# Two modulation chunks moved to the end of the experts, modulation started during the last merges, output weights loaded later

## The chip, the cores and the metric

The kernel runs on one core of a Trainium2 chip. The core has a matrix engine (TensorE, PE in the profile), a vector engine (VectorE, DVE), a scalar engine (ScalarE, ACT), GpSimd (POOL) and SyncE (SP). Each has its own queue of instructions, taken in order, and they meet through semaphores; 16 DMA engines move data between the core's memory and DRAM. SP issues most of the loads here, POOL the modulation's. The metric is device microseconds for one execution, as the median of several.

## The reference, cut to what matters

Two layers work on 512 latent and 256 context tokens of width 1024. All is float32; the kernel splits the operands of its large products into a high and a low part and adds three products.

```python
m_lat = jnp.split((sc @ ada_w[i] + ada_b[i])[:, None, :], 6, axis=-1)   # sc = silu(c)
m_ctx = jnp.split(scc @ ada_w[i] + ada_b[i], 6, axis=-1)                 # scc = silu(c_ctx)
h = modulate(rms_norm(x, norm_mix_w[i]), m[0], m[1])
y = hybrid_mixer(h)           # attention heads | gated delta rule, both ways; then @ w_out
x = x + m[2] * y
h = modulate(rms_norm(x, norm_ffn_w[i]), m[3], m[4])
x = x + m[5] * hier_moe(h)    # 32 experts, each token in two of them
```

`ada_w[i]` is 1024 x 6144 floats, 24 MB for a layer. The six chunks of 1024 columns are the m[0] to m[5] above. They depend on `c` and `c_ctx` alone, so they can be computed at any time before they are used: chunks 0 and 1 at the start of their layer, chunk 2 behind the mixer, 3 and 4 behind it, 5 behind the experts.

## The kernel before, in words

A layer runs in these stages, which the times of the first execution place as follows.

1. **Norm and input projection.** `norm_mix` modulates the tokens, transposes them and splits them into `hh` and `hl`. Products with the streamed `w_in` give `pn` (gates `gev`, queries, keys) and `pt` (delta rule's inputs). In layer 1 this begins at about 1112 us.
2. **Chunks and merges.** Each chunk of the delta rule needs the inverse of a small triangular matrix. It is built from 32x32 blocks; `merge_batch` joins them: 16 products of 32x32 into `mg` (L847), a ScalarE copy (L848), 16 products of the other kind (L851), a ScalarE copy into `xm` (L852), twice over, and a store of `xad`. The last merges stand directly ahead of the loop.
3. **The loop of 12 steps** (about 393 to 606 us in layer 0, 1461 to 1628 in layer 1). `delta_step` carries the state of the recurrence; `pz` (L917) is a step's first product. Each step's data (`lk`, `lx`, `lq`) are loaded one step ahead by SP; `lx` is multiplied with `lq` on POOL. Strings of letters (`PAT`) say in which order a step (d), slots of attention (f: scores `sc`, softmax `pp`, transposes `ptr`, product `pv`) and parts of the modulation (a) are written down. From that order and from its own model a scheduler sets each engine's order, which is then fixed.
4. **The tail**: output projection with `w_out` (raw loads `wr`, high parts `woh`), residual, norm, router.
5. **The experts**: 32 of them, weights streamed by SP three ahead through four buffers `w13` and two for the second matrix. Each result `ey` is added to `yd` in DRAM by an indirect DMA of POOL. Behind the last one the kernel branches over code for full experts, and the next layer loads `x` from `yd`.

**Modulation.** `ada_steps` does a chunk in four parts. A part (`ada_part`) loads 1 MB of `ada_w` into one of two buffers `araw` on POOL's queue, multiplies it on TensorE (8 products that the trace shows as 16, into `aps`), and copies the first part's sum on ScalarE or adds the others on VectorE (`ac`). After the fourth part the bias `ab` is added and the chunk stored to DRAM (`md`, L283), from where later stages load it. Layer 0's loop does chunks 2 to 5 of layer 0 and chunks 0 and 1 of layer 1, 24 parts; layer 1's loop does chunks 2 to 5 of layer 1, 16 parts, of which the scheduler puts one in front of the loop.

`WS` is the step from which on the raw output weights are loaded, one after each step, three in the loop; in the built order all three stand together behind the second steps' loads.

## Time and profile before

| | us |
|---|---|
| runs of the kernel before | 2085.26, 2092.97, 2104.73; median 2092.97 |
| profiled execution, its own time | 2092.51 |
| span of the profile | 2090.7 |
| TensorE busy | 1763.9 (84%) |
| VectorE busy | 1460.2 (70%) |
| ScalarE busy | 1016.6 (49%) |
| POOL busy | 868.6 (42%) |
| DMA | 427.81 MB, mean 205 GB/s |

The rows are read thus. A row of a timeline gives start, duration, engine, line, operation, what it writes <- what it reads, and how many instructions stand together; in brackets follow the idle time of that engine just before and what ended it. A row of waits adds such idle times by what ended them. A table of stretches gives each engine's busy time, the number of instructions and the granted clock of TensorE as a share of full speed. Idle time of one engine matters only where others wait for that engine.

### The profile page before, as it was taken

To read this page: it belongs to the slowest core of one execution; us is meant where nothing else is said; L and a number is where in the kernel's file an instruction comes from. 1 tells how busy PE (TensorE), PEld (TensorE's weight loads), DVE (VectorE), ACT (ScalarE), POOL (GpSimd) and SP (SyncE) were. 2 spreads that over 40 slices of the span, in tenths; PEclk is the share of its full clock that TensorE was granted. 3 is DMA by queue.
4 is the path that set the end of the run, shared out by engine and by line. 5 is a ranking of instruction groups with operands and counts; after the bars stand their busy time and mean duration, and the time that the engine had idled before them with its cause. 6 is when DMAs were issued, how large, how long until landed. Compare 5 with 4: busy or idle time off the path is not lost. (4 is left out here: it accounts for less than half of the span.)

```text
span 2090.7 us, 35600 instructions
## 1 busy us (share of the span) xinstructions
PE 1763.9 (84%) x13835; PEld 1382.1 (66%) x13835; DVE 1460.2 (70%) x2472; ACT 1016.6 (49%) x1595; POOL 868.6 (42%) x915
## 2 busy tenths in 40 slices
PE   6998798978877879999996987776898577999994
PEld 4887687766656746666665866675676465777773
DVE  4469996567673668887874579992678465787774
ACT  3444344665541246565554543343566225666663
POOL 4456653234354423343226466650234443334321
PEclk9999897799998979999997998875899788999997
DMA  9222445798645389998853323445983558988872
GB/s 283 74 71 82 129 119 166 218 259 246 205 125 144 147 327 336 332 322 301 324 161 119 97 73 97 131 130 158 282 233 83 148 214 315 346 334 330 328 295 102
DMA packets 227687, 427.81 MB, mean 205 GB/s; under 512 B 83720, under 2 KB 157180, under 8 KB 202939
## 3 DMA queue, kind: packets, MB, share of 16 engines
q1 hardware_dynamic: 171547, 329.09, 47.1%
q0 software_dynamic: 33536, 72.59, 12.2%
q10 hardware_dynamic: 22432, 23.81, 3.3%
q8 instruction: 111, 1.82, 0.4%
q14 instruction: 61, 0.50, 0.1%
HBM read 386.82 MB, written 84.67 MB: 226 GB/s over the span
## 5 line engine op out<-in xcount | busy, mean ns | idle before, releaser
L1418 POOL DMA_INDIRECT yd<-ey,idx x64 | 114.2, 1784 | 425.3 <-DMA yd<-ey,idx 151.8
L1364 PE MATMUL pab<-w,xt 128*128 128x512 f32 x512 | 230.3, 592 | 0.0
L1332 ACT ACTIVATE w2h<-w 128x2048 fp32r<-128x2048 f32 x64 | 122.7, 1917 | 134.5 <-PE py L1406 83.3
L1333 DVE TENSOR_TENSOR w2l<-w,w2h 128x2048 fp32r<-128x2048 f32 x64 | 146.8, 2294 | 53.5 <-ACT w2h L1332 52.9
L1333 DVE TENSOR_TENSOR w13l<-w,w13h 128x2048 fp32r<-128x2048 f32 x64 | 146.5, 2288 | 28.9 <-ACT w13h L1332 28.9
L1364 PEld LDWEIGHTS pab<-w,xt 128*128 128x128 f32 x512 | 93.0, 191 | 92.0 <-issue 91.8
L489 POOL TENSOR_TENSOR wlo<-wraw,whi 128x1024 fp32r<-128x1024 f32 (+1 forms) x44 | 111.1, 2529 | 93.1 <-ACT whi L488 93.1
L239 PE MATMUL pn<-whi,hh 128*128 128x256 f32 (+1 forms) x432 | 134.6, 314 | 16.3 <-ACT gev L1562 12.5
L239 PE MATMUL po<-woh,m 128*128 128x512 f32 x320 | 114.1, 434 | 30.7 <-ACT woh L1069 14.5
L239 PE MATMUL pn<-whi,hl 128*128 128x256 f32 (+1 forms) x432 | 135.3, 316 | 2.0 <-DVE hl L350 1.7
L239 PE MATMUL pn<-wlo,hh 128*128 128x256 f32 (+1 forms) x432 | 132.4, 308 | 1.2 <-POOL wlo L489 1.2
L1332 ACT ACTIVATE w13h<-w 128x2048 fp32r<-128x2048 f32 x64 | 121.8, 1902 | 6.4 <-DMA w<-w 4.1
L239 PE MATMUL pt<-hh,wlo 128*128 128x512 f32 (+1 forms) x352 | 124.2, 353 | 0.0
L239 PE MATMUL pt<-hh,whi 128*128 128x512 f32 (+1 forms) x352 | 122.9, 349 | 0.0
L239 PE MATMUL pt<-hl,whi 128*128 128x512 f32 (+1 forms) x352 | 122.2, 347 | 0.0
L1406 PE MATMUL py<-w2h,gh 128*128 128x512 f32 x256 | 109.1, 426 | 4.6 <-DVE ey L1413 4.4
L1337 POOL DMA_INDIRECT xe<-h2d,idx x64 | 85.9, 1343 | 61.2 <-issue 22.9
L518 DVE SCALAR_TENSOR_TENSOR dT<-xin,cw,dT 128x772 f32<-128x772 f32 x64 | 80.1, 1252 | 43.3 <-ACT dT L516 41.5
L1406 PE MATMUL py<-w2h,gl 128*128 128x512 f32 x256 | 103.1, 403 | 7.8 <-DVE gl L1385 7.8
L1413 DVE TENSOR_TENSOR ey<-py,eg 128x1024 f32<-128x1024 f32 x64 | 78.2, 1222 | 44.1 <-PE py L1406 37.8
L239 PEld LDWEIGHTS pn<-whi,hh 128*128 128x128 f32 x432 | 90.6, 211 | 23.2 <-ACT gev L1562 13.5
L1348 PEld LDWEIGHTS xt<-cst,xe 128*128 128x128 f32 x512 | 68.3, 192 | 55.1 <-issue 29.8
(401 smaller groups left out, 5124.4 us busy)
## 6 DMA issues: line engine op xcount, KB each, us to landing
w<-w SPq DMA_DIRECT2D x192, 1024.0 KB, 9.8
araw<-ada_w POOLq DMA_DIRECT2D x40, 1024.0 KB, 6.8
wraw<-w_in SPq DMA_DIRECT2D x40, 512.0 KB, 4.1
lk<-vk SPq DMA_DIRECT2D x48, 256.0 KB, 7.2
lx<-xad SPq DMA_DIRECT2D x40, 256.0 KB, 10.0
araw<-ada_w SPq DMA_DIRECT2D x8, 1024.0 KB, 10.9
wr<-w_out SPq DMA_DIRECT2D x8, 1024.0 KB, 13.4
vk<-vr ACTq DMA_DIRECT2D x16, 384.0 KB, 3.7
```

The costliest lines, as they stand in the source:

```text
L239: self.nc.tensor.matmul(ps, a(k), b(k), start=(first and n == 0), stop=(last and n == 3 * nk - 1))
L489: getattr(nc, eng).tensor_tensor(lo, raw, hi, op=OP.subtract)
L518: nc.vector.scalar_tensor_tensor(dst, xin[:, tap:tap + 772], cw[:, tap, f:f + 1], dst, op0=OP.mult, op1=OP.add)
L1332: self.pin(nc.scalar.activation(hi, src, AF.Copy))
L1333: self.pin(nc.vector.tensor_tensor(lo, src, hi, op=OP.subtract))
L1337: self.pin(self.nc.gpsimd.indirect_dma_start(out=xe, out_offset=None, in_=h2d, in_offset=bass.IndirectOffsetOnAxis(ap=idx, axis=0), bounds ...
L1348: pin(nc.tensor.transpose(ps[:, k * P:(k + 1) * P], xe.rearrange("p (q k) -> p k q", k=8)[:, 4 * q + k, :], self.ident))
L1364: self.pin(self.nc.tensor.matmul(out, xt[:, k, :], w13[:, :, KS + k, :], start=False, stop=(k == 3)))
L1406: pin(self.nc.tensor.matmul(py[:, n * 512:(n + 1) * 512], a[:, j, :], b[:, c], start=(j + m == 0), stop=(j == 1 and m == 2)))
L1413: pin(nc.vector.tensor_tensor(y, py, gates, op=OP.mult))
L1418: self.pin(self.nc.gpsimd.indirect_dma_start(out=yd, out_offset=bass.IndirectOffsetOnAxis(ap=idx, axis=0), in_=y, in_offset=None, bounds_c ...
```

## The change

It has three parts.

**`LATE = (2, 3)`.** Chunks 2 and 3 of layer 1 are no longer done in layer 1's loop. `ada_late` does them at the end of layer 0's experts: four loads of 2 MB each, as two of 1 MB, into the experts' `w13` buffers on SP's queue, issued as experts 28 to 31 release theirs; 64 products (eight parts' worth) into one tile, chunk 3 two rows below chunk 2 through a shifted copy of the small operand (`scs`); one ScalarE copy `la`. Two of the eight parts stand ahead of the last expert's second product, six behind it and ahead of the branch. `ada_close` then adds the biases in layer 1, behind `norm_mix`: for each chunk a small load `lb` (SP), a VectorE sum, a store to `md` (POOL). `md_row` finds chunk 3 two rows lower.

**`PRE = (6, 8)`.** Before the loop, six of layer 0's parts and all eight that are left in layer 1's are written down, so that the scheduler can place them beside the last merges. The strings `PAT` are the same; an "a" of an exhausted sequence does nothing.

**`WS = 7`.** The raw output weights are loaded from step 7 on, and each behind that step's `lx` load.

```diff
-WS = 4
+WS = 7
+PRE = (6, 8)
+LATE = (2, 3)
...
+    def ada_late(self, i, chs, pool, load):
...
+        acc = self.late_sum = pool.tile([P, UNIT], F32, tag="la", name="la")
...
+        for ch in chs:
+            for n in range(2):
+                raws.append(load(src[:, 4 * n:4 * n + 4, ch * D:(ch + 1) * D]))
+                yield
+        ps = self.psC("aps")
+        for j in range(2):
+            for k in range(8):
+                if k % 2 == 0:
+                    yield
+                for g in range(4):
+                    w = raws[2 * j + k // 4][:, k % 4, g * UNIT:(g + 1) * UNIT]
+                    self.pin(self.nc.tensor.matmul(ps[32 * g:32 * g + 32, :UNIT], self.scs[j][:, k, :], w, start=(j + k == 0), stop=(j == 1 and k == 7), tile_position=(0, 32 * g)))
+        self.pin(self.nc.scalar.activation(acc, ps[:, :UNIT], AF.Copy))
...
+    def ada_close(self, i, chs, pool):
...
+            ab = pool.tile([P, UNIT], F32, tag="lb%d" % ch, name="lb")
+            self.nc.sync.dma_start(ab, self.t["ada_b"][i, ch * D:(ch + 1) * D].rearrange("(g o j) -> g o j", g=4, o=1).to_broadcast([4, 32, UNIT]))
+            self.nc.vector.tensor_tensor(ab, self.late_sum, ab, op=OP.add)
+            getattr(self.nc, QUEUE["ada"]).dma_start(self.md[i][ch], ab)
...
             load(e + LA)
+            if e + LA >= NE:
+                next(late, None)
...
         out(NE - 2)
+        for _ in range(3):
+            next(late, None)
         down(NE - 1)
         out(NE - 1)
+        for _ in late:
+            pass
...
                     hh, hl = self.norm_first(rows, start, pool, hp) if i == 0 else self.norm_mix(i, rows, start, mod, pool, hp)
+                if i > 0:
+                    with self.pool("lb", B) as lb:
+                        self.ada_close(i, LATE, lb)
...
-                for l, ch in [(i, c) for c in range(2, 6)] + ([(i + 1, 0), (i + 1, 1)] if not last else []):
+                for l, ch in [(i, c) for c in range(2, 6) if i == 0 or c not in LATE] + ([(i + 1, 0), (i + 1, 1)] if not last else []):
...
+            for _ in range(PRE[i]):
+                next(ada, None)
...
-                        raws.append(self.wout_raw(i, len(raws), wrp.tile([P, 2 * D], F32, name="wr", tag="wr%d" % len(raws))))
+                        with tc.issue_after(self.stepx.ins):
+                            raws.append(self.wout_raw(i, len(raws), wrp.tile([P, 2 * D], F32, name="wr", tag="wr%d" % len(raws))))
```

Where the instructions then stand is told by the built order of three engines.

TensorE in layer 1, from the transposes `vt` to the end of the last merges, before:

```order
L985 MATMUL vt<-cst,vf 128x128 x6
L265 MATMUL aps<-araw,scp 32x256 x8
L847 MATMUL mg<-yt,uo 32x32 x32
L851 MATMUL mg<-yl,mg 32x32 x32
L847 MATMUL mg<-yl,uo 32x32 x32
L851 MATMUL mg<-yt,mg 32x32 x32
L847 MATMUL mg<-yt,uo 32x32 x32
L851 MATMUL mg<-yl,mg 32x32 x32
```

The same place after the change (lines are shifted by some 36 there):

```order
L270 MATMUL aps<-araw,scp 32x256 x8
L883 MATMUL mg<-yt,uo 32x32 x16
L270 MATMUL aps<-araw,scp 32x256 x8
L883 MATMUL mg<-yt,uo 32x32 x16
L887 MATMUL mg<-yl,mg 32x32 x32
L270 MATMUL aps<-araw,scp 32x256 x16
L883 MATMUL mg<-yl,uo 32x32 x32
L270 MATMUL aps<-araw,scp 32x256 x8
L887 MATMUL mg<-yt,mg 32x32 x16
L270 MATMUL aps<-araw,scp 32x256 x8
```

The piece ends within the third merge; two more parts follow before the first scores, one between the halves of each of the next two products. All eight parts that layer 1 still computes itself stand here, and none in its loop.

POOL at the start of layer 1, where the norm ends, before:

```order
L350 TENSOR_TENSOR hl<-nT,hh 128x256 x8
L507 MEMSET xin 128x2
L508 MEMSET xin 128x4
L509 MEMSET xin 128x2
...
L818 MEMSET sY 128x1024 x2
L1013 TENSOR_TENSOR gev<-gev,dw 128x256 x2
```

and after the change:

```order
L386 TENSOR_TENSOR hl<-nT,hh 128x256 x8
L854 MEMSET sY 128x1024 x2
L855 MEMSET sY 128x32 x2
L319 DMA md_2_84<-lb 128x256
L319 DMA md_3_85<-lb 128x256
L543 MEMSET xin 128x2
...
L1049 TENSOR_TENSOR gev<-gev,dw 128x256 x3
```

Two stores of modulation chunks now stand between the norm's last instruction and the first gate tile. The tiles `lb` lie where the norm's pool was, and the first gate tile lies where `lb` was: so the loads of `lb` wait for the last `hl`, and the first `gev` waits for both stores.

SP in layer 0's loop, around the loads of the output weights, before:

```order
L864 DMA lk<-vk_88 64x1024
L865 DMA lx<-xad_89 64x1024
L869 DMA lq<-qkd_90 64x512 x4
L1062 DMA wr<-w_out 128x2x1024 x3
L864 DMA lk<-vk_88 64x1024 x2
L865 DMA lx<-xad_89 64x1024 x2
```

and after the change, some 20 rows later in this queue:

```order
L901 DMA lx<-xad_89 64x1024 x2
L1098 DMA wr<-w_out 128x2x1024
L905 DMA lq<-qkd_90 64x512 x2
L900 DMA lk<-vk_88 64x1024 x2
L901 DMA lx<-xad_89 64x1024 x2
L1098 DMA wr<-w_out 128x2x1024
```

The three loads no longer stand ahead of the third step's data, but singly behind the `lx` loads of three late steps.

## Rows read from the trace of the kernel before

**Rows 1.** Stretches: us, busy time (instructions) of each engine, granted clock, DMA, GB/s.
```profile
core 0: us, PE busy (x) PEld busy (x) DVE busy (x) ACT busy (x) POOL busy (x), PEclk, DMA share, GB/s
344.00:393.00 49.00, 40.71 (x427) 34.56 (x427) 19.96 (x55) 33.33 (x80) 8.25 (x11) 0.51 0.58 177
...
1403.00:1461.00 58.00, 39.25 (x542) 34.33 (x542) 20.62 (x41) 24.69 (x43) 7.93 (x8) 0.53 0.61 176
1461.00:1500.00 39.00, 32.48 (x461) 25.04 (x461) 26.03 (x54) 22.48 (x44) 8.42 (x11) 0.87 0.96 286
1500.00:1570.00 70.00, 62.89 (x966) 47.02 (x964) 49.81 (x104) 42.43 (x81) 23.30 (x29) 0.98 0.84 235
```
**Rows 2.** Stretches, the modulation parts (`aps`) alone, in layer 1's loop.
```profile
1461.00:1500.00 39.00, 5.35 (x80) 2.17 (x80) 1.67 (x4) 0.36 (x1) 0.87 0.96 286
1500.00:1570.00 70.00, 10.86 (x144) 4.25 (x144) 2.92 (x7) 0.78 (x2) 0.98 0.84 235
```
**Rows 3.** Waits of TensorE in layer 1's loop: us in total, times, longest.
```profile
PE aps L265 <- DMA araw<-ada_w: 10.6, 6, 3.5
```
**Rows 4.** Timeline of TensorE, first products of steps in layer 1's loop.
```profile
1461.24 0.45 PE L917 MATMUL pz<-lk,lx 64*64 64x64 f32 x2 [0.23 <-DMA lx<-xad]
...
1579.55 1.15 PE L917 MATMUL pz<-lk,lx 64*64 64x64 f32 x32
...
1605.12 1.15 PE L917 MATMUL pz<-lk,lx 64*64 64x64 f32 x32
```
**Rows 5.** Timeline of TensorE in the last merges of layer 1.
```profile
1417.33 1.94 PE L265 MATMUL aps<-araw,scp 128*32 128x256 f32 x16
...
1423.21 1.86 PE L847 MATMUL mg<-yt,uo 32*32 32x32 f32 x32 [2.54 <-ACT mg L848]
...
1433.21 1.88 PE L847 MATMUL mg<-yl,uo 32*32 32x32 f32 x32 [2.91 <-DMA yl<-dy]
1435.84 1.91 PE L847 MATMUL mg<-yl,uo 32*32 32x32 f32 x32 [0.74 <-ACT mg L848]
...
1454.37 0.79 PE L604 MATMUL sc<-ka,qs 128*128 128x512 f32 x1 [0.68 <-ACT xm L852]
```
**Rows 6.** DMA issues: KB each, median us to landing; 1403 to 1461, then 393 to 430.
```profile
araw<-ada_w POOLq DMA_DIRECT2D x3, 1024.0 KB, 6.5
...
araw<-ada_w POOLq DMA_DIRECT2D x4, 1024.0 KB, 11.2
wr<-w_out SPq DMA_DIRECT2D x3, 1024.0 KB, 13.4
```
**Rows 7.** Start of layer 1: timeline, then a DMA row and two tile rows (ns).
```profile
1146.47 0.73 POOL L350 TENSOR_TENSOR hl<-nT,hh 128x256 fp32r<-128x256 f32 x1 [1.26 <-ACT hh L348]
1147.24 0.94 ACT L1010 ACTIVATE gev<-pn 128x256 f32<-128x256 f32 x3 [0.84 <-POOL hl L350]
1148.36 0.40 PE L239 MATMUL pn<-whi,hh 128*128 128x288 f32 x1 [0.70 <-ACT ba L1566]
...
xad<-dd SPq DMA_DIRECT2D x12, 256.0 KB, 2.6
...
L282 DVE TENSOR_TENSOR ac<-ac,ab x4: 415/420/425, 1486.2 to 1572.7; 128x256 f32<-128x256 f32 x4
L283 POOL DMA_DIRECT2D md<-ac x4: 595/599/602, 1486.9 to 1573.4; - x4
```
**Rows 8.** Waits in layer 0's loop, of TensorE and of POOL.
```profile
PE aps L265 <- DMA araw<-ada_w: 13.1, 5, 6.1
PE pz L917 <- DVE pl L638: 5.8, 1, 5.8
...
POOL lx L870 <- DMA lx<-xad: 14.9, 1, 14.9
```
**Rows 9.** Timeline of TensorE at the end of layer 0's experts.
```profile
1098.16 0.47 PE L1406 MATMUL py<-w2h,gh 128*128 128x512 f32 x1 [2.21 <-DVE ey L1413]
...
1118.37 0.91 PE L343 MATMUL nps<-cst,x 128*128 128x128 f32 x3 [13.94 <-DVE x L332]
```

More of the change, by code (lines that the diff above doesn't have):

```diff
@@ L250, in cond @@
         nc.vector.tensor_scalar(cc, cc, 0.5, None, op0=OP.mult)
-        sc = self.cp.tile([P, 8, 32], F32, name="scp")
-        nc.vector.memset(sc, 0.0)
+        pad = self.cp.tile([P, 260], F32, name="scp")
+        nc.vector.memset(pad, 0.0)
+        self.scs = [pad[:, 2 - 2 * j:258 - 2 * j].rearrange("p (k r) -> p k r", k=8) for j in range(2)]
+        sc = self.scs[0]
+        self.mdrow = {}
         nc.vector.scalar_tensor_tensor(sc[:, :, 0:2], th, 1.0, cc, op0=OP.add, op1=OP.mult)
@@ L284, in ada_steps @@
         yield
+    def ada_late(self, i, chs, pool, load):
+        if not chs:
+            return
+        acc = self.late_sum = pool.tile([P, UNIT], F32, tag="la", name="la")
+        src = self.t["ada_w"][i].rearrange("(p k) n -> p k n", k=8)
+        raws = []
+        for ch in chs:
[12 more added lines that the diff above has]
+    def ada_close(self, i, chs, pool):
+        for j, ch in enumerate(chs):
+            ab = pool.tile([P, UNIT], F32, tag="lb%d" % ch, name="lb")
+            self.nc.sync.dma_start(ab, self.t["ada_b"][i, ch * D:(ch + 1) * D].rearrange("(g o j) -> g o j", g=4, o=1).to_broadcast([4, 32, UNIT]))
+            self.nc.vector.tensor_tensor(ab, self.late_sum, ab, op=OP.add)
+            getattr(self.nc, QUEUE["ada"]).dma_start(self.md[i][ch], ab)
+            self.mdrow[i, ch] = 2 * j
     def md_row(self, i, ch, v):
-        return self.md[i][ch].rearrange("(o g r) j -> r o g j", o=1, g=4)[v].to_broadcast([P, 4, UNIT])
+        return self.md[i][ch].rearrange("(o g r) j -> r o g j", o=1, g=4)[v + self.mdrow.get((i, ch), 0)].to_broadcast([P, 4, UNIT])
     def mod_load(self, i, pool):
@@ L864, in step_load @@
             self.q("step").dma_start(k[rows[d]], vk[tl[d], rows[d]])
-            self.q("step").dma_start(x[rows[d], :np_], xad[tl[d], d, rows[d], :np_])
+            self.stepx = self.q("step").dma_start(x[rows[d], :np_], xad[tl[d], d, rows[d], :np_])
         if need:
@@ L1105, in logit_shift @@
         for g in range(4):
-            nc.sync.dma_start(m[32 * g:32 * g + 32], self.md[i][3][32 * g + v].rearrange("(p k) -> p k", k=8))
+            nc.sync.dma_start(m[32 * g:32 * g + 32], self.md[i][3][32 * g + v + self.mdrow.get((i, 3), 0)].rearrange("(p k) -> p k", k=8))
         mb = pool.tile([P, 8, P], F32, tag="h2T", bufs=1, name="mb")
@@ L1324, in expert_load, with half_load @@
         return w
+    def half_load(self, src, pool):
+        w = pool.tile([P, 2, 8, FF], F32, tag="w13", bufs=RB, name="w13").rearrange("p a k f -> p (a k f)").rearrange("p (k n) -> p k n", k=4)
+        for n in range(2):
+            self.nc.sync.dma_start(w[:, 2 * n:2 * n + 2], src[:, 2 * n:2 * n + 2])
+        return w
     def split(self, src, name, pool):
@@ L1419, in expert_add, with experts @@
                                                    bounds_check=ntok - 1, oob_is_err=False, compute_op=OP.add))
-    def experts(self, i, R, js, g5, h2d, yd, ntok, xw):
+    def experts(self, i, R, js, g5, h2d, yd, ntok, xw, late):
         nc, tc = self.nc, self.tc
@@ L1471, in experts @@
         xes = []
+        late = self.ada_late(min(i + 1, DEPTH - 1), late, R["pool"], lambda src: self.half_load(src, xw))
         self.pins(True)
@@ L1681, in layer @@
         rt = self.route_open(T, rp)
+        rt["pool"] = rp
         route = lambda n, lg: self.route_pair(rt, n, [tt - t0 for tt in tiles[n:n + 2]], lg, n == T - 2, tl)
@@ L1705, in layer @@
                 xw = xws.enter_context(self.pool("xw", A))
-                ex = self.experts(i, rt, [tt - t0 for tt in tiles], g5, h2d, yd, ntok, xw)
+                ex = self.experts(i, rt, [tt - t0 for tt in tiles], g5, h2d, yd, ntok, xw, () if last else LATE)
                 next(ex)
```

## The prediction

> **What bounds the kernel now.** I read the table of stretches first [rows 1, 2], because the page's shares are means over stages with different limits. In the loop of layer 1 (1461 to 1628) TensorE is busy 32.5 of 39 us and then 62.9 of 70, DMA is at 0.96 and 0.84, and the modulation parts take 5.35 and 10.86 us of TensorE's time: 15 parts of 1.07 us. In the merges ahead of it (1403 to 1461) the granted clock is 0.53, about the lower of its two levels (1.2 of 2.4 GHz), and TensorE is busy 39.3 of 58 us: it waits between short pieces for ScalarE's copies. So a part costs 1.94 us there [rows 5] and 1.07 in the loop (5.35 us are 80 products, 16 for a part [rows 2]). Next the waits of TensorE by releaser: in layer 1's loop 10.6 us for a modulation weight [rows 3], in layer 0's 13.1 us for one and 5.8 us at a first product `pz`, while POOL stood 14.9 us at a step's `lx` [rows 8]. Last the lines of time at the three seams that the change touches: the merges [rows 5], the end of layer 0's experts [rows 9] and the start of layer 1 [rows 7].
>
> **The sum** is made against the profiled execution: span 2090.7 us, time 2092.51, practically the median of 2092.97.
>
> *Layer 1's loop, 15 parts leave it.* Upper bound of the gain: their TensorE time and all waits for their weights, 5.35 + 10.86 + 10.6 = 26.8 us [rows 2, 3]. Lower bound: what a step takes that has no part. From 1579.55 to 1605.12 are two such steps, 12.8 us each; the eight steps from 1461.24 to 1579.55 took 118.3, and at 12.8 they take 102.3, a gain of 16.0 [rows 4]. The lower bound is nearer, since those steps have the same recurrence with its ScalarE and VectorE links; but the early steps' long waits for weights sit in one chain with the recurrence, and 12.8 still holds other waits. I take **-20**. The three 1 MB loads of output weights, formerly issued together at the loop's start, now go one each into the three steps after the seventh, where there are no modulation loads left: nothing, covered by a DMA system at 0.84 and less behind 1500 [rows 1]. Without that cover one such load costs a step at most what three did in layer 0, 5.8 us.
>
> *Layer 1's merges, seven more parts.* One part stood there already; the order puts the other seven between halves of merges, each right behind a piece after which TensorE waits for a copy. Cost if all the time is added: 7 x 1.94 = 13.6. What they fill: the parts behind the first halves fall into gaps of 2.54, 2.91 and several of 0.68 to 0.74 [rows 5]; a part fills at most its own 1.94 of the first, the pair of parts ahead of the load of `yl` all of the second, the others short ones: 1.9 + 2.9 + 4 x 0.7 = 7.6. Net **+6**. Ends: -10 (the clock rises, rival A) and +20 (the weights are late, rival B). The ScalarE copy and VectorE sums behind each part (0.42 us) lie beside the merges, where VectorE is busy 20.6 of 58 us [rows 1].
>
> *Start of layer 1, the bias of the two moved chunks.* The small tiles for it reuse the memory of the norm's pool, and the gate tiles `gev` reuse theirs. So a chain now stands between two instructions that followed each other at once: last `hl` on POOL ends at 1147.20, first `gev` on ScalarE starts 1147.24 [rows 7]. In between come: two issues on SP and a small load, two VectorE sums, two issues on POOL, and the landing of the stores. Nearest rows: a small transfer lands in 2.6, the sum is 0.42, the issue on POOL 0.60 [rows 7]. 2.6 + 0.4 + 2 x 0.6 + 2.6 = 6.8, with something for SP's issue: **+7**. TensorE can't hide it: at 1148.36 it already waits 0.70 for ScalarE to empty a buffer of `pn` [rows 7], so it stops a microsecond after. Behind the stores on POOL stand the small memsets of `xin` and the `gev` products, which wait for the same stores anyway. Ends: 5 (the first sum's store overlaps wholly) and 10.
>
> *End of layer 0's experts, eight parts.* Two go into TensorE's gap of 2.21 us ahead of the last expert's second product, six behind it, into 13.94 us of idle time that waits for the scatters and the reload of `x` [rows 9]. At the high clock the two take 2.1 us (nothing), at the low one 3.9, which makes the last scatter 1.7 late. The six are 6.4 to 11.6 us, ending before the reload. The 8 MB of weights come over SP, where the last expert's second weights now stand behind 2 MB of them; DMA is mostly free there, but the order of one queue is kept, and the scatters share the engines. Branch, `la` copy and the small weight loads behind the branch wait for the last part: a microsecond at most. **+2**, between 0 and +6. If the cover goes (scatters earlier), the six parts cost up to 11.6.
>
> *Layer 0's loop, six parts ahead of it and the output weights later.* Output weights first: three loads landing in 13.4 us went out between the loads of two steps [rows 6]; the `lx` behind them kept POOL 14.9 us and `pz` 5.8 [rows 8]. That wait goes; next late there are the modulation weights, which still share the time. Of their 13.1 us of waits some go too, as 18 parts remain where 24 were. The most that can go is 13.1 + 5.8 = 18.9; I take half, about 10, because two buffers still serve the parts and both layers' early steps load their own data. Given back: six parts at 1.94 instead of 1.07 us is 5.2, but attention work goes the other way, from the low clock into the loop, so +2. Net **-8**; ends -17 and +4.
>
> -20 + 6 + 7 + 2 - 8 = **-13**: 2092.5 - 13 = 2079.5, I say **2080**, own range 2064 to 2092.
>
> **Rivals.** *A, the merges speed up.* With the gaps filled TensorE gets the high clock there: twelve pieces of 1.9 us shrink by 1 - 1.07/1.94 = 0.45, 10 us, and the parts by 7 x 0.87 = 6, so +6 becomes -10; with -24 in the loop, nearer its upper bound, and -12 in layer 0, where six parts run ahead too: -24 - 10 + 7 + 2 - 12 = -37: **2055**. For it: gaps of about 0.7 us at a clock of 0.53 [rows 1, 5] look like too little work; against it: the merge pieces are 32x32, and 344 to 393 in layer 0 shows 40.7 of 49 us busy at a clock of 0.51 [rows 1]. Chance 0.22. The Trainium skill, "TensorE: Matmul & The Clock Gate", Part 1, says that an engine kept busy is given the full clock and an idle one half of it. By that rule A is what filled gaps would bring; the trace does not bear it out for the merges of layer 0.
>
> *B, the weights come late: slower.* The parts stand in TensorE's queue in order, with two buffers; a load can go out only when the part two before it is done. At 6.5 us to land, as in the merges now, a pair of parts comes every 6.5 + 3.9 = 10.4 us, three pairs after the first in 31 us, within the 37 from the one part now at 1417 to the scores at 1454 [rows 5, 6]. At 11.2 us, as in the loaded start of layer 0's loop, three take 45 us, and at the output weights' 13.4 us 52 us [rows 6]. The point from which it decides is thus about 8.5 us. At 13.4 the merges of layer 1 get 15 us longer on top of +6, layer 0's two pairs about 10 on top of its term, and `yl` and `xad`, behind which merges wait, come later too. -20 + 21 + 7 + 2 + 2 + 5 = +17: **2110**. For it: in layer 0 the same stretch already has a DMA share of 0.58 [rows 1] with small packets; against it, 6.5 us was measured among just these. Chance 0.12. The Trainium skill, "DMA: Bandwidth & Descriptors", Issuing engines are not separate DMA queues, says that transfers issued by different engines run on the same 16 DMA engines and interleave; by that rule POOL's weight loads and SP's merge traffic slow each other, and the two landings above agree.
>
> *C, the parts only filled waits in the loop.* The step is bound by the recurrence's chain of ScalarE and VectorE; then the gain in layer 1 is about 8 and 4 in layer 0: -8 + 6 + 7 + 2 - 4 = +3, **2095**. For it: TensorE sits 6.5 of 39 us and 7.1 of 70 idle [rows 1], not for weights alone; against: 12.8 us in steps without parts [rows 4]. Chance 0.21.
>
> **Numbers.** Forecast 0.45, A 0.22, C 0.21, B 0.12. About 1%, 21 us, can be told from no change here: faster means below 2072, slower above 2114. Faster: A and the low end of the forecast, 0.22 + 0.08 = 0.30. Slower: the upper part of B, 0.05. No change 0.65. The range leaves out the outer part of A and of B: **2054 to 2104**.
>
> **What would show it.** Right: steps of layer 1 near 12.5 us from the first on, no waits for modulation weights there, a first `pz` some 13 us later in its layer than now (7 at its start and 6 in the merges), TensorE standing about 7 us at `pn` behind the last `hl`, and `lx` in layer 0 without the 14.9. Wrong: a clock near 1 in the merges (A), waits of `aps` for weights ahead of the first `pz` (B), step lengths unchanged (C). A late last scatter of layer 0 would show the experts' end underpriced.

## The result, and the profile after

The change makes the kernel slower: the median of four runs is 2126.3 us (2118.37 to 2129.22) against 2091.86 us (2085.26 to 2104.73, also four); the ratio is 1.0143, 95% interval 1.0102 to 1.0183. (Ratios, here and below, are those recorded with their intervals; the quotient of the two medians is 1.0165.) One execution below, 2376.40 us in the ninth experiment at a granted clock of 0.69, was in a slow state of the chip and is left out. Forecast were 2080 us and a range that ends at 2104. The profiled execution has a span of 2125.6 us, 34.9 more than the one before. First two lines of the page, span and busy time of each engine (TensorE's 1792.7 us are 84% of the span):

```profile
span 2125.6 us, 35594 instructions
PE 1792.7 (84%) x13835; PEld 1403.1 (66%) x13835; DVE 1457.5 (69%) x2466; ACT 1015.2 (48%) x1594; POOL 845.6 (40%) x905
```

To see where the time went, I cut both profiled executions at the same eleven instructions (first `pz`, first output product `po`, first expert's `xt` and so on) and subtracted; every entry is a difference of two start times on a timeline. The last column is one more execution of the kernel before; its stages differ by up to 5 us from the first's.

| stage, ending at | before, us | change after | predicted | before, taken again |
|---|---|---|---|---|
| first `pz` of layer 0 | 393.3 | +11.4 | | -0.3 |
| first `po` of layer 0 | 211.7 | +12.5 | both: -8 | +0.2 |
| first expert's `xt` | 143.1 | -2.5 | 0 | -4.9 |
| last `py` | 353.3 | -2.7 | 0 | -5.0 |
| first `nps` of layer 1 (experts' end) | 17.0 | +6.7 | +2 | +0.4 |
| first `gev` (start of layer 1) | 28.9 | +8.8 | +7 | 0 |
| first `pz` of layer 1 (merges) | 314.0 | +13.6 | +6 | -0.8 |
| last `pz` (layer 1's loop) | 163.2 | -12.2 | -20 | +4.2 |
| last `py` of layer 1, three more stages | 441.0 | -0.9 | 0 | -1.5 |

So one term has the wrong sign and 32 of the 48 us by which the sum missed: layer 0. The others have the sign that was forecast, and each came out on the bad side.

A single pair of executions measures a stage only roughly. Three versions below (bias tiles early, dummy parts, a quarter of the late weights) leave layer 0 as the change has it, with the same instructions up to its first `pz` in the same order; they show +1.9, +7.1 and +8.0 in the first row of the table and +12.9, +7.4 and +13.7 in the second. Four others leave layer 0 as it was before; their two rows together show +0.6, +5.3, +4.7 and +2.2. So the change costs layer 0 some 14 to 24 us, and the profile shown here lies at the upper end.

The stretches after, columns as in [rows 1]: the last 61 us ahead of the first `pz` of layer 0, the next 65 us, the whole loop, and of it the modulation parts (`aps`) alone (without a column for POOL); then the merges of layer 1 and its loop.

```profile
344.00:405.00 61.00, 43.23 (x534) 32.34 (x530) 17.38 (x47) 30.00 (x69) 14.43 (x19) 0.60 0.78 233
405.00:470.00 65.00, 45.34 (x674) 32.85 (x676) 32.03 (x73) 23.65 (x60) 24.88 (x29) 0.72 0.83 230
404.70:628.90 224.20, 183.26 (x2609) 140.50 (x2609) 154.16 (x324) 126.96 (x251) 90.52 (x93) 0.87 0.66 184
404.70:628.90 224.20, 23.59 (x288) 8.74 (x288) 5.81 (x14) 1.52 (x4) 0.87 0.66 184
...
1430.00:1509.00 79.00, 52.43 (x702) 39.75 (x702) 27.42 (x58) 27.27 (x46) 16.16 (x19) 0.55 0.69 211
1509.20:1659.10 149.90, 128.75 (x1919) 105.11 (x1918) 116.20 (x235) 96.88 (x181) 43.01 (x40) 0.92 0.45 116
```

Whole loops of the kernel before in the same view, layer 0's and layer 1's, and of each the parts alone:

```profile
393.30:605.00 211.70, 174.96 (x2685) 132.92 (x2684) 145.94 (x313) 119.41 (x233) 90.03 (x99) 0.93 0.77 224
393.30:605.00 211.70, 28.85 (x384) 11.35 (x384) 7.45 (x18) 2.29 (x6) 0.93 0.77 224
1461.20:1623.40 162.20, 140.05 (x2158) 108.33 (x2158) 119.97 (x251) 97.40 (x184) 55.68 (x60) 0.95 0.70 197
1461.20:1623.40 162.20, 17.28 (x240) 6.91 (x240) 5.00 (x12) 1.14 (x3) 0.95 0.70 197
```

**Layer 0 first.** Waits of TensorE after, in total, times and longest: for the parts' weights from 344 to 405, from 405 to 470, and in the loop (404 to 617); then POOL's for `lx` in the loop:

```profile
PE aps L270 <- DMA araw<-ada_w: 7.3, 3, 3.4
...
PE aps L270 <- DMA araw<-ada_w: 15.6, 3, 8.1
...
PE aps L270 <- DMA araw<-ada_w: 22.9, 5, 8.1
...
POOL lx L906 <- DMA lx<-xad: 33.5, 7, 7.5
```

and POOL's for `lx` in the loop before:

```profile
POOL lx L870 <- DMA lx<-xad: 49.4, 8, 14.9
```

POOL's waits fell by 16 us and its longest by half, as the step on `lx` said [rows 8]; TensorE's for weights rose from 13.1 to 22.9 us inside the loop, with 7.3 more ahead of it. The landing of such a load, median of the eight issued from 344 to 405, is the first line here; below it those issued in the merges of layer 1, and the small loads of merged halves beside them (columns as in [rows 6]):

```profile
araw<-ada_w POOLq DMA_DIRECT2D x8, 1024.0 KB, 12.6
...
araw<-ada_w POOLq DMA_DIRECT2D x8, 1024.0 KB, 7.1
...
yl<-dy SPq DMA_DIRECT2D x8, 128.0 KB, 12.0
```

Rival B's mechanism, parts that wait for their weights, holds in layer 0 and not in layer 1: 12.6 us to land in the one, 7.1 in the other. (The 8.5 us from which B decides were worked out for the spacing in layer 1's merges; for layer 0 the waits above show it directly.) In the stretch with the longest of these waits the granted clock is 0.72 (405 to 470), and over the loop 0.87 against 0.93; the products other than the parts take 183.26 - 23.59 = 159.7 us (2321 of them) where 2301 took 174.96 - 28.85 = 146.1. So the loop's +12.5 are 8.3 us more of busy time, in spite of six parts fewer, and 4.2 of idle time.

**The seams.** Timeline of TensorE after: seven of the eight parts at the experts' end (the trace shows one, at 1115.73, and not two ahead of the last expert's second product), the first `nps` behind them, and in the merges of layer 1 a wait for `yl`.

```profile
1120.94 6.25 PE L310 MATMUL aps<-w,scp 128*32 128x256 f32 x112
...
1143.86 0.88 PE L379 MATMUL nps<-cst,x 128*128 128x128 f32 x3 [15.94 <-DVE x L368]
...
1444.42 1.03 PE L883 MATMUL mg<-yl,uo 32*32 32x32 f32 x16 [12.33 <-DMA yl<-dy]
```

and the chain at the start of layer 1 on POOL, SP, POOL and ScalarE, with the issues of `araw` and `yl` (POOL, SP) behind it:

```profile
1172.67 0.73 POOL L386 TENSOR_TENSOR hl<-nT,hh 128x256 fp32r<-128x256 f32 x1 [1.27 <-ACT hh L384]
1173.43 1.31 SPq L317 DMA_DIRECT2D lb<-ada_b  x2
1178.78 1.28 POOL L319 DMA_DIRECT2D md<-lb  x2 [3.38 <-issue]
1181.61 0.94 ACT L1046 ACTIVATE gev<-pn 128x256 f32<-128x256 f32 x3 [9.02 <-DMA md<-lb]
...
1431.63 1.49 POOL L233 DMA_DIRECT2D araw<-ada_w  x2
1432.16 0.99 SPq L870 DMA_DIRECT2D yl<-dy  x2
```

Last `hl` and first `gev`, 0.04 us apart before [rows 7], now have 8.2 us between them (1173.40 to 1181.61). In the merges no part waits for its weights; but two 1 MB loads go out half a microsecond ahead of two loads of `yl`, 128 KB each, and TensorE stands 12.33 us for these. In the last merges before, its longest wait for `yl` was 2.91 [rows 5], but at another product: the order of the whole stage is another after the change.

The stage of +13.6 has two pieces. All eight parts stand behind the last `vt` transposes. From these to the first `pz`, before and after:

```profile
1417.00:1461.20 44.20, 29.14 (x416) 24.94 (x414) 7.37 (x17) 13.93 (x24) 0.74 (x1) 0.54 0.49 140
```

```profile
1459.40:1509.20 49.80, 39.97 (x529) 28.32 (x528) 10.24 (x24) 14.77 (x26) 6.24 (x9) 0.57 0.77 242
```

This piece is 5.6 us longer: seven more parts, of which idle time (15.1 us before, 9.8 after) takes up 5.2. The other 8 us lie ahead of the last `vt`, where no part stands and where the wait of 12.33 is.

### The profile page after: what moved, and what is told of

Same layout as the page of the kernel before. It is cut to its first block, busy times and chain, and to the rows that moved or that the text cites. A ratio compares the mean times of both kernels' runs of the same rounds, so it can differ in the third digit from the quotient of the medians.

```text
span 2125.6 us, 35594 instructions
## 1 busy us (share of the span) xinstructions
PE 1792.7 (84%) x13835; PEld 1403.1 (66%) x13835; DVE 1457.5 (69%) x2466; ACT 1015.2 (48%) x1594; POOL 845.6 (40%) x905
## 5 line engine op out<-in xcount | busy, mean ns | idle before, releaser
L241 PE MATMUL po<-woh,m 128*128 128x512 f32 x320 | 111.7, 426 | 20.3 <-ACT m L1077 11.4
```

Of the source, the lines that this page charges most:

```text
L241: self.nc.tensor.matmul(ps, a(k), b(k), start=(first and n == 0), stop=(last and n == 3 * nk - 1))
```

## The experiments

All ratios are to the kernel before on the same chip. The first four do one part of the change each, with the scheduler left to order the rest; the next four alter the whole change; then two put parts together, one spreads the output weights, and one is the kernel before again. Where a text speaks of a theory: for layer 0, that the weights come late or that attention is pushed back; for the experts' end, that the scatters are slowed by the loads; for the merges, that `yl` comes behind `araw`; for the output weights, that their place beside the last modulation loads matters; for layer 1's loop, that parts only filled waits (a rival of the prediction) or kept up the clock.

**Output weights from the eighth step on, alone.**

```diff
-PRE = (6, 8)
+PRE = (0, 0)
-LATE = (2, 3)
+LATE = ()
```

> Only the output weights go later (from step 7, each behind that step's lx); modulation as before. Theory 1 (the slowdown in layer 0 comes from the six parts ahead of its loop): the 14.9 us stall of lx and the 5.8 us at pz go, total 2082 to 2092, first pz of layer 0 within 1 us of before, last pz of layer 0 up to 8 us earlier. Rival (the later output weights do the harm, by colliding with late steps and the tail): 2100 or more, with the tail of layer 0 some 7 us longer.

Measured 2116.02 us, ratio 1.0103 (1.0072 to 1.0134), in the rival's range. The steps ahead of the moved loads are up to 11.6 us earlier, yet the loop of layer 0 takes 16.7 us more. The three go out on SP at 509.42, 525.04 and 551.18. The stretch behind the third:

```profile
556.00:571.00 15.00, 7.76 (x102) 5.28 (x102) 6.10 (x12) 5.05 (x9) 3.19 (x4) 0.82 1.01 262
```

In layer 0 the modulation loads run to the late steps: there is no cover. Parts wait 5.22 us at 532.29 and 6.45 at 569.92; with DMA at 1.01 TensorE is busy 7.76 of 15 us. These waits are not the whole price, though: over the loop those for weights are 14.6 us where they were 13.1. TensorE is also busy 9.5 us longer, at a clock of 0.88 for 0.93, and waits 9.6 us for the recurrence's state `S`, where it waited 0.4. The 5.8 us at `pz` are gone, as the prediction said, and this wait stands in their place; where it comes from is shown with the experiment that spreads the three loads, which has the same order of instructions.

**Two chunks at the experts' end, alone.**

```diff
-WS = 7
-PRE = (6, 8)
+WS = 4
+PRE = (0, 0)
-                        with tc.issue_after(self.stepx.ins):
+                        if True:
```

> Only chunks 2 and 3 of layer 1 go to the end of layer 0's experts; nothing is taken ahead of the loops, output weights as before. Theory 1: layer 0 as before up to its experts, then +4 to +7 at the experts' end and +9 to +10 at the first gate tile of layer 1, and 7 to 12 off layer 1's loop, from 8 parts less: 2094 to 2100. Rival (the move is worth its price): 2085 or less, with the two seams under 8 us together.

Measured 2112.47 us, 1.0115 (1.0052 to 1.0178), above what either theory gave. Both seams are there as in the whole change: +7.8 at the experts' end, +8.2 at the start of layer 1. What was to pay for them is not: with eight of its 15 parts fewer, layer 1's loop is 3.7 us longer. Loop and parts alone:

```profile
1476.40:1642.20 165.80, 139.52 (x2031) 110.54 (x2030) 119.95 (x243) 97.53 (x182) 47.94 (x48) 0.89 0.51 140
1476.40:1642.20 165.80, 8.36 (x112) 3.26 (x112) 2.50 (x6) 0.38 (x1) 0.89 0.51 140
```

The other products take 139.52 - 8.36 = 131.2 us at a clock of 0.89, where they took 140.05 - 17.28 = 122.8 at 0.95. DMA fell from 0.70 to 0.51, yet TensorE still waits 7.4 us for the weights of the seven parts that are left (10.6 before [rows 3]).

**Six parts ahead of layer 0's loop, alone.**

```diff
-WS = 7
-PRE = (6, 8)
+WS = 4
+PRE = (6, 0)
-LATE = (2, 3)
+LATE = ()
-                        with tc.issue_after(self.stepx.ins):
+                        if True:
```

> Only six parts of layer 0's modulation are taken ahead of its loop; everything else as before. Theory 1: the first pz comes about 11 us later, the loop's first steps wait for modulation weights, the tail is longer, and layer 0 reaches its first expert about 20 us (15 to 25) late: 2107 to 2117. Rival (they are harmless by themselves, harm comes with the other parts): within 5 us of before, 2087 to 2097.

Measured 2113.38 us, 1.0107 (1.0057 to 1.0158): +11.4 to the first `pz` and +7.6 in the loop. TensorE's waits from 344 to 617:

```profile
PE aps L270 <- DMA araw<-ada_w: 29.1, 5, 12.7
```

This alone makes the first +11.4 of the whole change; with the +7.6 it is nearly all of the 20.2 us by which this span is longer.

**Eight parts ahead of layer 1's loop, alone.** The same edit with `PRE = (0, 8)`.

> Only layer 1 takes eight of its 16 parts ahead of its loop; the other eight stay in the loop. Theory 1: the two 1 MB weight loads that go out ahead of the stores and loads of the first late merge make that merge wait for yl (12.3 us in the changed kernel), +10 to +12 at the first pz of layer 1; the loop gives back 8 to 12: 2088 to 2096. Rival (the merges hide the parts): first pz at most 6 later, loop 12 to 16 shorter, 2080 to 2086.

Measured 2103.16 us, 1.0029 (1.0007 to 1.0052): the cheapest of the four. +10.9 in the merges against -2.9 in the loop. The theory's 10 to 12 at the first `pz` came true by luck: it was to come from a wait of 12.3 us for `yl`, and here, in nearly the order of the kernel before, the longest for `yl` is 3.9 (3.9 before, too). What costs here are the parts. From the last `vt` to the first `pz`:

```profile
1418.60:1473.90 55.30, 44.45 (x553) 30.53 (x551) 13.30 (x29) 17.46 (x31) 9.96 (x14) 0.56 0.85 266
```

Nine parts stand in it where one stood; it is 11.1 us longer than before, and its idle time, 10.9 us for 15.1, took up only 4.2 of them. The four ratios add to 3.5%, more than the 1.4% of the whole: they are not independent, since each part of the change also alters the order that the scheduler finds for the rest (from first `gev` to first `pz` of layer 1 the first three show +4.1, +6.4 and +5.2 us, though nothing is changed there, and the kernel before, taken again, -0.8).

**The bias tiles of the moved chunks taken up ahead of the norm.**

```diff
-                with self.pool("nm", B) as pool:
-                    ...
                 if i > 0:
                     with self.pool("lb", B) as lb:
                         self.ada_close(i, LATE, lb)
+                with self.pool("nm", B) as pool:
+                    ...
```

> The changed kernel, but the biases of the two moved chunks are added and stored ahead of layer 1's norm instead of behind it, so that no memory is handed from the norm over lb to gev. Theory 1 (the chain over lb costs what the trace shows): the first gev follows the last hl at once again, 8 to 10 us less: 2116 to 2119. Rival (the wait was hidden or turns up elsewhere): within 3 us of the changed kernel, 2123 to 2129.

Measured 2119.21 us, 1.0104 (1.0079 to 1.0130), 7 us below the whole change's median, which is from another chip. ScalarE at the start of layer 1:

```profile
1167.31 0.94 ACT L1046 ACTIVATE gev<-pn 128x256 f32<-128x256 f32 x3 [0.84 <-POOL hl L386]
```

The 9.02 us are 0.84 again, the releaser is again `hl`, and that stage goes from +8.8 to -1.6; 3.8 us of it are given back ahead of `nps`. The cause of this term is shown.

**Dummy parts in layer 1's loop.** Sixteen parts shaped like the real ones are added to the whole change; they multiply data that lies in SBUF, load nothing, and their sums go unused.

```diff
             def modulation():
+                if last:
+                    for _ in range(16):
+                        ps = self.psC("aps")
+                        for r in range(2):
+                            for g in range(4):
+                                ...matmul(ps[32 * g:32 * g + 32, :UNIT], self.sc[:, r, :], dT[0][:, g, 0:UNIT], ...)
+                        yield
```

> The changed kernel, with 16 parts of TensorE products on data that lie in the core anyway (no loads, their sums unused) put where layer 1's loop had its modulation parts: 17 us more work for TensorE. Theory C' (the parts used to stand in waits and kept TensorE's clock up; the emptied loop runs at a granted clock of 0.91 instead of 0.95, and the same other work takes 133 us busy instead of 126): the clock of the loop rises to 0.95 or more, the busy time of the other products falls by 5 us or more, and the loop from first to last pz stays at 151 us or gets up to 5 shorter. Rival (the loop is bound by TensorE's work, so every part counts): the loop gets 12 to 17 us longer, 163 to 168, and the total as much.

Measured 2140.12 us, 1.0195 (1.0165 to 1.0224). The loop, and the dummy parts in it:

```profile
1512.00:1666.40 154.40, 138.05 (x2160) 106.81 (x2159) 117.58 (x235) 96.64 (x180) 42.98 (x40) 0.95 0.43 115
1512.00:1666.40 154.40, 17.29 (x240) 6.48 (x240) 0.00 (x0) 0.00 (x0) 0.95 0.43 115
```

Fifteen of the sixteen stand in the loop, one ahead of it. 17.29 us of products that nobody needs make the loop 4.5 us longer (149.9 to 154.4): the clock is back from 0.92 to 0.95, and the other products take 120.8 us instead of 128.75. The theory on the clock was right on clock and products, a little wrong on the loop, which it had as unchanged or shorter; its rival's +12 to +17 did not come. Two limits. Six executions with an emptied loop (the change, the versions with early bias tiles, with a quarter of the weights and without loads, and the two that put parts together) take 147.9 to 151.0 us from first to last `pz`, at clocks of 0.92 to 0.95; by the same measure this loop takes 155.3, so 4 to 7 more. And its instructions stand in another order than the change's, so what the dummies do to the clock is not parted from what the order does. The run as a whole is 14 us slower than the change, of which the stage ahead of the loop has 9.6 in this execution, with the change's order of instructions but for the one dummy part; what took them is not shown.

**A quarter of the late weights.** Only 256 of each chunk's 1024 columns are loaded at the experts' end, 2 MB for 8, and all products read these; the two chunks' values are not the reference's.

```diff
-                    w = raws[2 * j + k // 4][:, k % 4, g * UNIT:(g + 1) * UNIT]
+                    w = raws[2 * j + k // 4][:, k % 4, 0:UNIT]
...
-            self.nc.sync.dma_start(w[:, 2 * n:2 * n + 2], src[:, 2 * n:2 * n + 2])
+            self.nc.sync.dma_start(w[:, 2 * n:2 * n + 2, 0:UNIT], src[:, 2 * n:2 * n + 2, 0:UNIT])
```

> The changed kernel, but the late chunks' loads at the end of layer 0's experts bring a quarter of the columns (2 MB instead of 8 MB; the products read this quarter four times, so these two chunks are not the reference's). Theory 2 (the loads share the DMA engines with the scatters, which follow one another at 10.6 instead of 7.5 to 9.9 us, and so end later): the last scatter starts within 5 us of the last expert product again (9.9 in the changed kernel, 3 to 4 before), total 4 to 7 us less than the changed kernel, 2119 to 2122. Rival (the products, the copy la and the small loads behind the branch hold up the start of layer 1): unchanged seam, 2124 to 2129.

Measured 2121.69 us, 1.0111 (1.0067 to 1.0155). The last scatters of layer 0's experts on POOL, of the whole change, of the kernel before, and here:

```profile
1104.47 1.68 POOL L1461 DMA_INDIRECT yd<-ey,idx  x1 [8.87 <-DMA yd<-ey,idx]
1115.03 1.54 POOL L1461 DMA_INDIRECT yd<-ey,idx  x1 [8.88 <-issue]
1124.19 1.54 POOL L1461 DMA_INDIRECT yd<-ey,idx  x1 [7.61 <-DMA yd<-ey,idx]
1130.86 1.54 POOL L1461 DMA_INDIRECT yd<-ey,idx  x1 [5.12 <-issue]
```

```profile
1088.39 3.52 POOL L1418 DMA_INDIRECT yd<-ey,idx  x1 [5.46 <-DVE ey L1413]
1098.29 1.54 POOL L1418 DMA_INDIRECT yd<-ey,idx  x1 [6.38 <-DVE ey L1413]
1105.79 1.54 POOL L1418 DMA_INDIRECT yd<-ey,idx  x1 [5.96 <-issue]
```

```profile
1111.84 2.29 POOL L1461 DMA_INDIRECT yd<-ey,idx  x1 [5.25 <-DVE w2l L1376]
1120.31 1.54 POOL L1461 DMA_INDIRECT yd<-ey,idx  x1 [6.18 <-DMA yd<-ey,idx]
1127.01 1.54 POOL L1461 DMA_INDIRECT yd<-ey,idx  x1 [5.16 <-issue]
```

After the change the scatters wait for one another. Beside the 8 MB they follow each other at up to 10.6 us and are still behind when the last product ends (1121.0); the last starts 9.9 us later. Before, the experts' loads ended earlier, the scatters came at 7.5 to 9.9 us and caught up: they waited for `ey`, not for each other, and the last started 3.1 us behind the last product (1102.7). With 2 MB the seam is +1.6 in place of +6.7. That the loads slow the scatters is shown in this stage; for the whole time the 4.6 us between the medians are within what runs differ by.

**Layer 0's six early parts without their loads.** They multiply data that lies in SBUF. The chunk's values are then other ones, other experts' blocks run, and the time (2511.08 us) compares with nothing; the trace is read up to the first expert.

```diff
-        raw = self.wload(pool, src[:, 2 * n:2 * n + 2, ch * D:(ch + 1) * D], bufs, "araw", q=q)
+        raw = None if dry is not None else self.wload(pool, src[:, 2 * n:2 * n + 2, ch * D:(ch + 1) * D], bufs, "araw", q=q)
...
```

> The changed kernel, but the six parts ahead of layer 0's loop multiply data that lie in the core instead of loading 6 MB of weights (one chunk and a half of layer 0 are then not the reference's). Theory 1a (what hurts layer 0 is that the weights come late): first pz 5 to 8 us earlier than in the changed kernel, the first five steps 10 to 14 us shorter, first expert at most 10 us behind the kernel before: 2108 to 2116. Rival 1b (what hurts is that attention is pushed out of the merges to the end of the loop): the first steps may be quicker, but the output projection still starts 8 us or more after the step end, and the first expert stays 15 to 20 late: 2120 to 2126.

The first `pz` comes 4.2 us later than before, not 11.4, and the loop is 2.8 longer, not 12.5. Waits for weights in the loop:

```profile
PE aps L271 <- DMA araw<-ada_w: 12.2, 5, 3.2
```

So 4.2 + 2.8 = 7 us are left without the loads, little more than the +0.6 to +5.3 of versions with layer 0 unchanged, where four executions with them show +14.5 to +23.9: 7 to 17 us hang on the loads. A limit: in the whole change only 8 of 80 score products of attention stand ahead of the first `pz` (12 before), and more attention work runs late in the loop; here it is 11. Without loads the scheduler chose another order, so how these divide between waiting and pushed attention stays open.

**The two chunks at the experts' end, bias early, eight parts ahead of layer 1's loop; layer 0 as before.**

```diff
-WS = 7
-PRE = (6, 8)
+WS = 4
+PRE = (0, 8)
```

(with the moved bias tiles and without `issue_after`, as above)

> Layer 0 and the output weights as in the kernel before; chunks 2 and 3 of layer 1 at the experts' end, with their biases ahead of the norm; all eight other parts of layer 1 ahead of its loop. Stage by stage from the runs so far: layer 0 +0 (its 21 us came from the parts ahead of its loop and from the later output weights, theory 1), experts' end +7, first gate tile 0, projection and merges +11 to +14, loop -12: 5 to 9 us over the kernel before, 2098 to 2106. Rival (the parts help each other in the changed kernel, so that taking two out leaves layer 0 slow or layer 1's gain away): 2115 or more.

Measured 2109.80 us, the median of six, 1.0082 (1.0055 to 1.0110), between the two ranges that were expected. The first 24 us of layer 0 are mostly gone (-1.0 and +5.7), the loop of layer 1 is 14.7 us shorter; the experts' end (+11.3) and the merges (+19.0) take it back. TensorE's wait in the merges:

```profile
PE mg L883 <- DMA yl<-dy: 12.6, 1, 12.6
```

**The same, with the first two weight loads behind `yl`.**

```diff
-            for _ in range(PRE[i]):
-                next(ada, None)
+            for n in range(PRE[i]):
+                self.first_q = "sync" if i > 0 and n < 2 else None
+                with tc.issue_after(self.yl1.ins):
+                    next(ada, None)
...
```

> As e9, but the first two modulation loads of layer 1 (2 MB) go out on SP's queue behind the loads yl of the merge that waited, instead of on POOL's queue beside them. Theory 3 (these 2 MB slow the small yl loads from 3 to 4 us to 12, and the merge waits 12.3): the wait for yl falls to 4 us or less, the first pz of layer 1 comes 8 to 11 us earlier than in e9, total 2088 to 2096. Rival (yl is late by itself, or the parts then wait for their weights): gain under 3 us, with waits of aps for weights in the merges in place of that for yl.

Measured 2103.22 us, 1.0036 (1.0010 to 1.0061): 6.6 us less than the one before it, on the same chip, and above the 2096 that the theory gave at most. SP's queue and the waits:

```profile
1416.74 1.09 SPq L233 DMA_DIRECT2D araw<-ada_w  x2
```

```profile
PE mg L883 <- DMA yl<-dy: 6.7, 1, 6.7
PE aps L270 <- DMA araw<-ada_w: 3.5, 4, 1.3
```

The wait fell from 12.6 to 6.7 us, and the stage by 8 us. So about half of the wait came from the two loads ahead of `yl`; that is shown. The other half did not go. Two versions that take no part ahead of layer 1's loop, the two late chunks alone and layer 0's six parts alone, have nearly the change's order there and issue their two loads just behind `yl`, too. TensorE waits 6.87 us in the one, and in the other:

```profile
1417.54 1.03 PE L883 MATMUL mg<-yl,uo 32*32 32x32 f32 x16 [7.56 <-DMA yl<-dy]
```

From the first `gev` to the last `vt` these two are +7.3 and +6.9 us, the change +8.1. (The profiled execution of this experiment, at 2092.09 us, was near its fastest; the stages are read from it, the verdict from the median.)

**Output weights from the fifth step on as before, but one for each step.**

```diff
-WS = 7
-PRE = (6, 8)
+WS = 4
+PRE = (0, 0)
-LATE = (2, 3)
+LATE = ()
```

> The kernel before, but its three loads of output weights go one behind the lx loads of each of the steps that follow the fourth, instead of all three ahead of the third step's data (modulation as before). Theory 4 (the burst at the loop's start costs 6 to 8 us, and in e1 the loads fell on the last modulation loads of layer 0, which cost 15 to 20): the early gain stays, the late loss is gone, 4 to 8 us under the kernel before. Rival (any place in layer 0's loop collides with modulation loads): the waits of aps come at steps 5 to 8 instead, 0 to 10 us over the kernel before.

Measured 2106.98 us, 1.0065 (1.0037 to 1.0093), above both ranges; the loop of layer 0 is 7.9 us longer. Waits from 400 to 620, then a wait of VectorE and one of TensorE in the loop:

```profile
POOL lx L906 <- DMA lx<-xad: 32.5, 6, 7.6
...
PE aps L270 <- DMA araw<-ada_w: 11.7, 7, 3.7
```

```profile
417.08 0.42 DVE L692 TENSOR_TENSOR fu<-pv,pvt 64x256 f32<-64x256 f32 x1 [8.04 <-DMA atd<-fu]
...
418.22 2.07 PE L934 MATMUL pq<-S,dT 64*64 64x64 f32 x28 [6.61 <-DVE S L975]
```

POOL stands 17 us less for `lx` than before and TensorE 1.4 us less for weights, the 5.8 us at `pz` are gone, and the loop does not gain. VectorE's order is another: an attention result `fu` stands ahead of the state `S` here, behind it in the kernel before. `fu` waits 8.04 us for the store (`atd`) of an earlier one, and TensorE 6.61 us for `S`, and 3.7 more a little later. The first experiment has the same order on every engine but SP, and the same waits (7.76 and 6.33). So the edit brought another order with it, and whether spreading the loads under the old order would gain something stays untested. What the two show side by side is the place of the loads alone: late, the loop takes 8.8 us more than spread, of which 5.3 are busy time of TensorE and 2.9 waits for weights.

**The kernel before, once more.**

> The kernel before once more, to see how much its stages differ between two profiled executions. Expected: first pz of layer 0 within 3 us, every stage within 4 us of the first profile; if layer 1's projection and merges (first gate tile to first pz, 314 us) came 4 to 6 us longer here too, the 4 to 6 us that all variants show there are no effect of any change.

One execution of 2084.77 us, without an edit; it gives the last column of the table above. Two of its stages miss the expected 4 us by a little (-4.9, -5.0), and the merges came out at -0.8: the +4 to +6 that versions show there without an edit there come with their order of instructions.

No version was faster than the kernel before; the nearest, eight parts ahead of layer 1's loop alone at 1.0029, has an interval that begins at 1.0007.

## Why the prediction was wrong

**Layer 0: the step that failed.** "-8" was half of waits that might go, plus 2 for the early parts. Measured: +23.9 in this pair, +14.5 to +23.9 over four executions. First, the waits counted as gain: those at `lx` and `pz` did go, but with the output weights late (+16.7) or only spread (+7.9) the loop did not shorten, since the scheduler's new order put a wait of 6.3 to 6.6 us for `S` in their place, and with parts ahead of the loop those for weights grew from 13.1 to 22.9. Second, the decisive one: the loads of the early parts were taken at no price, though the prediction itself had a landing of 11.2 us there [rows 6]. It put rival B, at 0.12, into the merges of layer 1, where 6.5 us had been measured, and gave layer 0 only a side term of it. 12.6 us were measured in layer 0, with waits of 7.3 us ahead of the loop; without the loads 7 of the 14 to 24 us are left. Third, the sentence "where there are no modulation loads left" was written for layer 1's loop and holds there; in layer 0 the same edit moved the three loads onto the last modulation loads, 8.8 us more than in the early steps when done alone.

**Layer 1's loop: right sign, somewhat too large.** -12.2 for -20 in this pair. Five executions with all parts in the loop take 163.2 to 167.8 us, of which the first profile is the shortest, six with none 147.9 to 151.0, of which the change's is the longest: 12 to 20 us, and 16 between the middle ones, which is the lower bound that the prediction worked out [rows 4] before it took 20. (The 15 parts took 17.28 us, 1.15 each; its 5.35 + 10.86 are 14 of them.) That steps with no part take 12.8 us was measured while other steps, with parts, kept TensorE busy around them. Emptied of parts, the loop's other products take 126.1 to 129.8 us in the six executions, for 122.5 to 124.8: 1 to 7 us given back. Adding the parts' time back (dummy parts) returns 4 to 7 us of the gain; the rest goes with the loads, the waits for them (10.6 us [rows 3]) and the order. Rival C's step, that the parts only filled waits, was more than half right for the products, but its 8 us lie outside of what these executions show.

**Merges: +13.6 for +6**, inside the ends -10 and +20. For the piece that the sum describes, the last merges, it was right: +5.6 behind the last `vt`, the price of a part 1.94 us, no part waited. That its parts fill 7.6 us is not so well borne out: idle time fell by 5.2 here and by 4.2 in the version with these parts alone. The other 8 us lie ahead of this piece and have no term in the sum. Versions that move no part there show 7 of them in nearly the same order of instructions, so most of it came with the order. The new loads ahead of `yl` make TensorE's wait 12.33 us where it is 6.7 to 7.6 with the loads behind; the prediction named this ("`yl` and `xad` come later too") and gave it no price. It is worth 1 us of the stage against those versions and 8 between the two that put parts together, so its size stays open. The Trainium skill ("DMA: Bandwidth & Descriptors", Issuing engines are not separate DMA queues), cited with rival B, says that transfers started by different engines interleave on the same 16 DMA engines. The trace agrees: the loads ahead of `yl` go out on POOL's queue at 1431.63, `yl` on SP's at 1432.16, and the wait is the 12.33 us.

Rival A did not come. The Trainium skill ("TensorE: Matmul & The Clock Gate", Part 1) says that the clock is held back by default and that activity releases it. The trace does not bear that out for the merges: with seven more parts behind the last `vt`, TensorE busy 39.97 of 49.8 us, the clock is 0.57 (0.54 before).

**Start of layer 1: right.** +8.8 for +7, inside 5 to 10; 8.2 us between `hl` and `gev`, and taking the tiles up earlier removes it.

**Experts' end: +6.7 for +2**, just outside 0 to +6. The eight parts cost nothing (1.07 and 6.25 us at full clock inside idle time), as said. What was late next was the scatters, at up to 10.6 us each beside the loads. "The scatters share the engines" was in the step, without a row for a scatter beside a load; there were such rows, from the experts' middle, 11.0 and 12.3 us apart (1041.07, 1053.32, 1064.32 in the trace before).

## What to carry over

Before filling a gap with work that needs a load, price the load in that very stretch: its landing there against the spacing of the work, and the small transfers that would be issued just behind it. A wait that goes is no gain by itself, since the next one may take its place; only a shorter stretch is. An edit to one place can bring another order of instructions everywhere, so a stage that was not edited has to be looked at, too, and one pair of executions is too little. And work that fills an engine's gaps can pay for part of itself: taking 17 us of it out of a loop gave 12 to 20, of which dummies took back only 4 to 7.

## Unexpected on the hardware

- 17.29 us of useless products in a loop of 150 us cost 4.5 us (4 to 7 against six executions of the emptied loop): the granted clock was 0.95 with them and 0.92 without, and the other products took 8 us less. The order in the loop was another, too.
- TensorE waited 12.33 us for two loads of 128 KB issued half a microsecond behind two of 1 MB on another queue; with the large ones issued behind them, 6.7 to 7.6 in three versions.
- Chained accumulating scatters follow each other at 10.6 us beside streaming weights, and at 6.7 once these have ended.
- TensorE busy 52.4 of 79 us with mostly 32x32 products stays at a granted clock of 0.55, about the lower of its two levels.
- The same instructions in the same order up to the first `pz` reached it at 395.2 to 404.7 us in five executions.
